# A state-space mixer's taps and state outputs on 32-column tiles of TensorE

## The chip, the cores and the metric

The kernel runs on one core of one Trainium2 chip. The metric is the device time of one execution, in microseconds; three runs of the kernel before took 1072.55, 1073.31 and 1074.68 us, median 1073.31 us.

## What is computed

The program is two transformer blocks over 256 tokens of width 1024: two layers of a first block (a state-space mixer, a gated spatial mixer, a differential attention, a conv-gated MLP), then one layer of a second block with three attention branches. The change touches only the state-space mixer of the first block:

```
def s5_mixer(u, a_re, a_im, log_dt, b_re, b_im, c_re, c_im, d_skip, w_glu, b_glu):
    ...
    a_bar = jnp.exp(lam * dt)
    b_bar = ((a_bar - 1.0) / lam)[..., None] * b_mat
    bu = jnp.einsum("bsgh,gph->bsgp", uf.astype(jnp.complex64), b_bar)
    ...
    _, states = lax.associative_scan(combine, (a_seq, bu), axis=1)
    y = jnp.real(jnp.einsum("bsgp,ghp->bsgh", states, c_mat))
    y = y + d_skip.astype(jnp.float32).reshape(SSM_GROUPS, SSM_GROUP) * uf
    y = jax.nn.gelu(y.reshape(bsz, seq, SSM_WIDTH))
    y = y * jax.nn.sigmoid(y @ w_glu.astype(jnp.float32) + b_glu.astype(jnp.float32))
```

There are 256 channels in 16 groups of 16; each group has 64 complex states of its own, and groups don't mix before the last product.

## The kernel before, in words

All weights stream from memory once, in a fixed order of use (`Stream`, L98). ACT writes the upper part of a weight tile (`whi`, L152), DVE the rest (`wlo`, L153), and TensorE (PE) multiplies three times per tile (L94, the helper `Bank.mm`: `xh*whi`, `xh*wlo`, `xl*whi`). The order of the instructions on each engine is made by a scheduler when the kernel is built, from the order of the code and from priorities; it is fixed in the program, and no engine overtakes itself.

The mixer takes segments of 4 tokens. `ssm_prep` (once per layer) makes its constants. The layer-0 call runs beside the first products, the layer-1 call beside the layer-0 MLP. For each half `a` (128 of the 256 channels, four groups of 32 channels, numbered `q`) it

- writes the powers of A times B, padded with zeros, into a tile `pad`, one for the real and one for the imaginary part (two copies of ACT each, L600);
- transposes `pad` on PE (L603) and copies it out into `bt` (ACT, L604);
- multiplies `pad` by C into the four taps of 128x128 (`px<-sgen,sgen`, helper L94), of which only the four diagonal blocks of 32x32 are not zero by construction and are kept: four copies of ACT into `ktap` (L616), and one DVE instruction that adds the skip term (L617).

All of this goes through one PSUM bank, `px` (a pool of one), so each step waits until the step before has been copied out.

`ssm_gen` runs the mixer: 16 small transfers spread the input over partitions (L896, queue SP), PE makes what each segment adds (L905), DVE scans over segments (L920) and makes the state before each segment (L409, L929). Then two sets of products go into one PSUM bank: taps times inputs (`acc<-ut,ktap`), and states times `ct` (`acc<-sgen,ct`, 64 products per layer, which the trace shows as 128 instructions). Each of the latter has 32 weight columns, writes 32 rows of the bank (`yv[rows, ...]`), and so takes one of four column tiles of PE. Their loop has the group `q` outside, and the tap `i` and the part `ri` inside, so eight products in a row go to the same column tile:

```
for q in range(4):
    rows = slice(q * 32, q * 32 + 32)
    j = a * 4 + q
    for i in range(4):
        for ri in range(2):
            yb.mm(yv[rows, a, i, :], ct[:, i, ri, j * 32 : j * 32 + 32], st_[ri][:, j, :],
```

ACT's gelu (L948) reads that bank when all are done, and PE's next step of the mixer (L954, the gate) reads the gelu.

The whole program is PE's 7751 matmul instructions and their weight loads, at 96% busy. A product of two fp32 operands stands in the trace as two instructions, one that is written with fp32r operands (the weight stream) as one.

Of the kernel before, what the change touches and what calls it, by code (L numbers as in the profile page):

```python
# [20 lines left out]
P = 128  # L21
# [18 lines left out]
# columns of the transposed parameter rows  # L40
AG, FG, GP, GM, SG, SD, BG, BM, AR, AI, GV, NPV = 0, 16, 32, 40, 48, 50, 54, 58, 82, 98, 114, 118
# columns of the constant table
# [3 lines left out]
def constant_table():  # L46
    """Rotary tables, masks: functions of shapes only. Tokens of block 2 stand in the order
    (t mod 4, t div 4 mod 4, t div 16)."""
# [30 lines left out]
@contextmanager  # L79
def later(tc, n):  # L80
    """Scheduled as if traced n instructions later."""
    tc.cur_priority += n
    yield
    tc.cur_priority -= n


class Bank:
    """One PSUM bank, whose accumulation groups share one start and one stop."""
# [4 lines left out]
    def mm(self, out, lhsT, rhs, stop=False):  # L93
        self.nc.tensor.matmul(out, lhsT=lhsT, rhs=rhs, start=not self.open, stop=stop)  # L94
        self.open = True


class Stream:  # L98
    """The weights in the order of their use: loaded, and split into two float32r parts, ahead of it."""
# [67 lines left out]
def tile_model(tc, t, out):  # L167
# [54 lines left out]
    # ------------------------------------------------------------------ weights in order of use  # L222
# [12 lines left out]
    # products of the mixers (lower case) and their generators' steps  # L235
# [58 lines left out]
    # ------------------------------------------------------------------ constants and small inputs  # L294
# [15 lines left out]
    def param_rows(*ps, eng=nc.sync):  # L310
        """Parameter rows -> columns of pvt."""
# [57 lines left out]
    # ------------------------------------------------------------------ small numeric helpers  # L369
    def rsqrt(src, n, scale, dst=None, tag=None):  # L370
        """1 / sqrt(src * scale + EPS) for a [P, n] tile."""
# [35 lines left out]
    # ------------------------------------------------------------------ first block: SSM parameters  # L407
# [12 lines left out]
    def ssm_params():  # L420
# [27 lines left out]
        # half angle -> full angle, then onto the unit circle  # L448
# [14 lines left out]
        # f = (a_bar - 1) / lambda  # L463
# [28 lines left out]
    def ssm_prep(l):  # L492
        """Segments of 4 tokens: A^i B-bar, C A^k, the 4-tap kernels Re(C A^i B-bar), the rotation table
        e^(-4 i theta m), m < 64, and the scan's multipliers."""
# [14 lines left out]
        def cmul(o, x, y, tv):  # L509
            """o = x * y for (re, im) pairs, tv scratch of o's shape."""  # L510
            tt(o[0], x[0], y[0], OP.mult)
            tt(tv, x[1], y[1], OP.mult)
            tt(o[0], o[0], tv, OP.subtract)
            tt(o[1], x[0], y[1], OP.mult)
            tt(tv, x[1], y[0], OP.mult)
            tt(o[1], o[1], tv, OP.add)
# [6 lines left out]
        # C^T, states on partitions, expanded with zeros and compact  # L523
# [15 lines left out]
        # powers of A, 0 to 4, and their products with f  # L539
# [23 lines left out]
        # C A^k, k from 1 to 4, the imaginary part negated  # L563
# [15 lines left out]
        # A^i B-bar; stacked as (channel, i) rows by states, and times C for the taps  # L579
# [12 lines left out]
        for a in range(2):  # L592
            pads = []
            for ri in range(2):
                pad = sgen()
                G.memset(pad, 0.0)
                pd = pad.rearrange("p (j h c i) -> p h j c i", j=4, i=4, h=2)
# [8 lines left out]
                yield  # L606
            kb = psx()
            for ri in range(2):
                cs = slice(ri * S + a * P, ri * S + (a + 1) * P)
                for i in range(4):  # L610
                    kb.mm(kb.t[:, i * P : (i + 1) * P], pads[ri].rearrange("p (k i) -> p k i", i=4)[:, :, i],
                          c0[:, cs], stop=ri == 1 and i == 3)
            kv = kb.t.rearrange("p (i c) -> p i c", i=4)
            for q in range(4):
                ps = slice(q * 32, q * 32 + 32)
                A.copy(ktap[ps, :, a, ps], kv[ps, :, ps])  # L616
# [3 lines left out]
        # rotation table  # L620
# [28 lines left out]
    # ------------------------------------------------------------------ token order of block 2  # L649
# [6 lines left out]
    # ------------------------------------------------------------------ normalisation helpers  # L656
# [5 lines left out]
    def split_scaled(hi, lo, src, scale):  # L662
        """hi + lo = src * scale, scale a [P, 1] column or a float."""
# [7 lines left out]
    class Stats:  # L671
        """Sums of squares over d (rows of the d-major tiles) per token."""
# [26 lines left out]
    def token_ss(src, n):  # L699
        """Sum of squares over the free axis of src[:, tt, :] (token-major), [P, 2]."""  # L700
# [11 lines left out]
    # ------------------------------------------------------------------ products  # L712
    low = [0]

    def mm_xs(X, banks, outs, sub, k0, kn, last):
        """Token-major: outs[tt] += X[:, k, tt].T @ W[k]."""
# [15 lines left out]
    def mm_ws(X, bank, outs, sub, k0, kn, last):  # L732
        """d-major: outs[n] += W[k][:, n].T @ X[:, k]."""
# [57 lines left out]
    # ------------------------------------------------------------------ x, its first norm  # L791
# [13 lines left out]
    # masks and rotary tables  # L805
# [11 lines left out]
    def rope_gain(pool, name, con, c0, s0, g, axes):  # L817
        """Tables with the norm's gain folded in: cos * g, and sin * (g of the other half)."""
# [68 lines left out]
    # ------------------------------------------------------------------ mixers of the first block  # L887
    def ssm_gen(l, ut, mix):
        tab, rr, bt, ct, wg = SSM[l]
        # ut: [P, (a, i, m)], token 4 m + i  # L890
# [3 lines left out]
        for q in range(4):  # L894
            for i in range(4):
                nc.sync.dma_start(u4v[3 - i : P : 4, q], utv[q * 32 : q * 32 + 32, :, i, :])  # L896
        yield
        w = [sgen(), sgen()]
        for a in range(2):
            # what each segment adds to its last state  # L900
# [21 lines left out]
        # state before each segment, from 0  # L922
# [15 lines left out]
        for a in range(2):  # L938
            for q in range(4):
                rows = slice(q * 32, q * 32 + 32)  # L940
                j = a * 4 + q
# [901 lines left out]
```

## Time and profile before

| | before |
|---|---|
| three runs, device time | 1072.55, 1073.31, 1074.68 us |
| span of the profiled execution (first to last instruction; the page gives no other time of it) | 1071.4 us |
| PE busy | 1028.5 us, 7751 instructions |
| DVE busy | 779.0 us |
| ACT busy | 624.1 us |
| DMA, mean over the span | 156 GB/s |

A busy time counts from an instruction's start to its end. PE's instructions overlap, and a wide one lasts 0.28 us though the next starts 0.12 us after it, so the distance of the starts, not the duration, says what an instruction costs. In the timeline a run of like instructions is one row, from the first start to the last end, with their number.

### The profile page before, as it was taken

The page shows a single profiled execution, that of the slowest core. Times are in us where ns is not written, and L with a number is a line of the kernel's source. Part 1 is how long each engine was busy: PE and PEld are TensorE (multiplying, and loading weights), DVE is VectorE, ACT ScalarE, POOL GpSimd, SP SyncE. Part 2 cuts the span into 40 slices and gives each one's busy share as a digit, 9 for nine tenths or more (in the row PEclk, how much of TensorE's full clock was granted, in tenths as well). Part 3 has the DMA queues.
Part 4 walks back from the last instruction along what each step waited for, and adds up shares of the span by engine and source line. Part 5 has one row for each costly group of instructions (what it writes and reads, how often), then busy time and mean ns, then how long its engine had stood idle before and what let it go on. Part 6 is the DMA issues. An engine that isn't in the chain of part 4 may idle for free.

```text
span 1071.4 us, 19616 instructions
## 1 busy us (share of the span) xinstructions
PE 1028.5 (96%) x7751; PEld 956.9 (89%) x7751; DVE 779.0 (73%) x1577; ACT 624.1 (58%) x1206; POOL 14.3 (1%) x34
## 2 busy tenths in 40 slices
PE   7799999999999999998999999999999999999994
PEld 5678898999999988888999999999787899899993
DVE  6978769877888769658878787876665666546663
ACT  5876567655665667657655555645675555444450
POOL 2000000000000000100000000000000000000000
PEclk9899999999999999999999999999999999999997
DMA  7542253555655445135556555468332546336531
GB/s 200 194 141 91 63 173 118 191 172 185 222 177 193 158 131 191 66 124 170 164 176 207 169 190 193 152 184 275 121 119 80 167 114 195 112 113 192 164 137 39
DMA packets 130484, 166.66 MB, mean 156 GB/s; under 512 B 12034, under 2 KB 103256, under 8 KB 130392
## 3 DMA queue, kind: packets, MB, share of 16 engines
q1 hardware_dynamic: 130360, 165.40, 47.9%
q8 instruction: 61, 1.00, 0.4%
q14 instruction: 31, 0.25, 0.1%
q10 hardware_dynamic: 32, 0.01, 0.0%
HBM read 160.15 MB, written 1.05 MB: 150 GB/s over the span
## 4 chain that ended last, share of the span: by engine, by line
PE 85%; DVE 7%; ACT 4%; issue 1%; DMA 1%; SPq 0%; POOL 0%; ACTq 0%; POOLq 0%; DVEq 0%
PE acc L94 50%; PE ps L94 26%; PE px L94 2%; DVE sgen L409 2%; DVE wlo L153 1%; PE pt L1506 1%; ACT sgen L600 1%; ACT whi L152 1%; ACT gen L1005 1%; PE px L905 1%; PE acc L1561 1%; DMA wraw<-in_w_in_dram 1%; PE acc L1652 1%; PE pt L1124 0%; DVE gen L1331 0%
## 5 line engine op out<-in xcount | busy, mean ns | idle before, releaser
L152 ACT ACTIVATE whi<-wraw 128x1024 fp32r<-128x1024 f32 x294 | 307.7, 1060 | 235.0 <-PE acc L94 112.5
L153 DVE TENSOR_TENSOR wlo<-wraw,whi 128x1024 fp32r<-128x1024 f32 x294 | 356.5, 1222 | 103.5 <-ACT whi L152 100.6
L94 PE MATMUL ps<-xh,whi 128*128 128x256 f32 x736 | 208.6, 285 | 3.7 <-DVE gen L1342 3.4
L94 PE MATMUL ps<-xl,whi 128*128 128x256 f32 x736 | 208.2, 283 | 0.8 <-DVE xl L665 0.8
L94 PE MATMUL ps<-xh,wlo 128*128 128x256 f32 x736 | 207.9, 283 | 0.0
L94 PE MATMUL acc<-xh,wlo 128*128 128x256 f32 x672 | 193.7, 289 | 4.0 <-DVE wlo L153 4.0
L94 PE MATMUL acc<-xh,whi 128*128 128x256 f32 x672 | 194.9, 291 | 1.2 <-ACT vm L1195 0.7
L94 PE MATMUL acc<-xl,whi 128*128 128x256 f32 x672 | 193.9, 289 | 0.5 <-DVE xl L669 0.5
L94 PEld LDWEIGHTS ps<-xh,whi 128*128 128x128 f32 x736 | 140.5, 191 | 4.4 <-DVE gen L1342 1.9
L94 PEld LDWEIGHTS ps<-xl,whi 128*128 128x128 f32 x736 | 140.8, 191 | 1.1 <-DVE xl L665 1.0
L94 PEld LDWEIGHTS ps<-xh,wlo 128*128 128x128 f32 x736 | 140.8, 191 | 0.0
L94 PEld LDWEIGHTS acc<-xh,wlo 128*128 128x128 f32 x672 | 129.6, 193 | 5.8 <-DVE wlo L153 4.7
L94 PEld LDWEIGHTS acc<-xh,whi 128*128 128x128 f32 x672 | 129.4, 193 | 4.7 <-issue 1.3
L94 PEld LDWEIGHTS acc<-xl,whi 128*128 128x128 f32 x672 | 129.5, 193 | 2.8 <-issue 1.5
L94 PE MATMUL acc<-whi,xh 128*128 128x512 f32 (+1 forms) x352 | 125.5, 358 | 3.0 <-ACT xh L664 2.6
L94 PE MATMUL acc<-wlo,xh 128*128 128x512 f32 (+1 forms) x352 | 125.8, 357 | 1.7 <-DVE wlo L153 1.6
L94 PE MATMUL acc<-whi,xl 128*128 128x512 f32 (+1 forms) x352 | 124.7, 355 | 0.0
L94 PE MATMUL acc<-al,whi 128*128 128x256 f32 x352 | 99.0, 281 | 0.5 <-DVE al L669 0.5
L94 PE MATMUL acc<-ah,whi 128*128 128x256 f32 x352 | 99.2, 282 | 0.0
L94 PE MATMUL acc<-ah,wlo 128*128 128x256 f32 x352 | 98.6, 281 | 0.0
L94 PEld LDWEIGHTS acc<-whi,xh 128*128 128x128 f32 x352 | 67.4, 191 | 11.7 <-ACT xh L664 3.5
L94 PEld LDWEIGHTS acc<-wlo,xh 128*128 128x128 f32 x352 | 67.4, 191 | 10.7 <-DVE wlo L153 2.6
(348 smaller groups left out, 1558.2 us busy)
## 6 DMA issues: line engine op xcount, KB each, us to landing
wraw<-in_w_in_dram SPq DMA_DIRECT2D x58, 1024.0 KB
wraw<-in_w_up_dram SPq DMA_DIRECT2D x44, 1024.0 KB
wraw<-in_w_down_dram SPq DMA_DIRECT2D x22, 1024.0 KB
wraw<-in_w_out_dram SPq DMA_DIRECT2D x12, 1024.0 KB
wraw<-in_w_mem_kv_dram SPq DMA_DIRECT2D x4, 1024.0 KB
gen<-gen SPq DMA_DIRECT2D x48, 64.0 KB
wraw<-in_w_br_b_dram SPq DMA_DIRECT2D x2, 1024.0 KB
wraw<-in_w_br_m_dram SPq DMA_DIRECT2D x2, 1024.0 KB
```

Source lines behind the costliest of these rows:

```text
L94: self.nc.tensor.matmul(out, lhsT=lhsT, rhs=rhs, start=not self.open, stop=stop)
L152: self.nc.scalar.activation(hv, part, AF.Copy)
L153: self.nc.vector.tensor_tensor(lv, part, hv.bitcast(F32), op=OP.subtract)
L409: (eng or V).tensor_tensor(o, a, b_, op=op)
L600: A.copy(pd[ps, hf], bpow[ri][ps, a * 4 : a * 4 + 4])
L905: T.matmul(bv[:, ri, q, :], lhsT=bt[:, ri, a, q * P : (q + 1) * P], rhs=u4[:, a * 4 + q, :], start=True, stop=True)
L1005: A.activation(sq[:, i * 64 : i * 64 + 64], src[:, i * 64 : i * 64 + 64], AF.Square, scale=rstd[:, q : q + 1], accum_out=ss[:, i : i + 1])
L1506: T.transpose(bk.t[:, i * P : (i + 1) * P], p[:, i * P : (i + 1) * P], ident)
L1561: T.matmul(oc, lhsT=pt[:, kt * P : (kt + 1) * P], rhs=vs[0][:, kt, cols], start=kt == 0, stop=False)
L1652: T.matmul(oc, lhsT=pt[:, (i * 2 + kt) * P : (i * 2 + kt + 1) * P], rhs=vb[:, kt, kv * 64 : kv * 64 + 64], start=kt == 0, stop=kt == 1)
```

## The change

The padded tile is laid out as (tap, channel) within each group of 32 channels, so that the 32 columns of one tap and one group lie side by side. The taps are made group by group: a product of 32 weight columns by 32 moving columns, written to the 32 rows of its group, with the four groups (column tiles) as neighbours. The state outputs get the same order: the group inside, tap and part outside. The 16 transfers of `ssm_gen` follow the new row order.

```
     def mm(self, out, lhsT, rhs, stop=False, start=None):
...
-                pd = pad.rearrange("p (j h c i) -> p h j c i", j=4, i=4, h=2)
+                pd = pad.rearrange("p (j i h c) -> p h j c i", j=4, i=4, h=2)
...
             kb = psx()
+            kv = kb.t[:, :P].rearrange("p (i c) -> p i c", i=4)
             for ri in range(2):
-                cs = slice(ri * S + a * P, ri * S + (a + 1) * P)
                 for i in range(4):
-                    kb.mm(kb.t[:, i * P : (i + 1) * P], pads[ri].rearrange("p (k i) -> p k i", i=4)[:, :, i],
-                          c0[:, cs], stop=ri == 1 and i == 3)
-            kv = kb.t.rearrange("p (i c) -> p i c", i=4)
+                    for q in range(4):
+                        ps = slice(q * 32, q * 32 + 32)
+                        c = ri * S + a * P + q * 32
+                        kb.mm(kv[ps, i, :], pads[ri][:, q * P + i * 32 : q * P + i * 32 + 32], c0[:, c : c + 32],
+                              start=ri == 0 and i == 0, stop=ri == 1 and i == 3)
             for q in range(4):
                 ps = slice(q * 32, q * 32 + 32)
-                A.copy(ktap[ps, :, a, ps], kv[ps, :, ps])
+                A.copy(ktap[ps, :, a, ps], kv[ps])
...
-                nc.sync.dma_start(u4v[3 - i : P : 4, q], utv[q * 32 : q * 32 + 32, :, i, :])
+                nc.sync.dma_start(u4v[(3 - i) * 32 : (4 - i) * 32, q], utv[q * 32 : q * 32 + 32, :, i, :])
...
         for a in range(2):
-            for q in range(4):
-                rows = slice(q * 32, q * 32 + 32)
-                j = a * 4 + q
-                for i in range(4):
-                    for ri in range(2):
-                        yb.mm(yv[rows, a, i, :], ct[:, i, ri, j * 32 : j * 32 + 32], st_[ri][:, j, :],
+            for i in range(4):
+                for ri in range(2):
+
+                    for q in range(4):
+                        j = a * 4 + q
+                        yb.mm(yv[q * 32 : q * 32 + 32, a, i, :], ct[:, i, ri, j * 32 : j * 32 + 32], st_[ri][:, j, :],
                               stop=a == 1 and i == 3 and ri == 1)
```

The rest of the diff takes comments out and shifts later line numbers by three.

**What moves.** Counted over the program, 32 products of 128x128 give way to 128 of 32x32 on PE, and the 16 copies L600 of ACT get another shape; every other instruction is there as before. The scheduler moves some: on PE all but two blocks of the differences lie between rows 179 and 500, the mixers of layer 0 (the two are the layer-1 taps); on DVE they lie between rows 196 and 546, on ACT between 62 and 244; on SP one load changes places, on POOL nothing does.

PE, the first taps of layer 0 (`px_642` is the bank of the taps, `px_660` and after the change `px_684` the next transposes through the same bank; an order row of x4 holds four products). Before:

```order
L94 MATMUL acc_895<-xh_160,wlo_709 128x256
L94 MATMUL px_642<-sgen_429,sgen_529 128x128 x4
L94 MATMUL px_642<-sgen_429,sgen_539 128x128 x4
L94 MATMUL acc_1026<-wlo_749,xh_160 128x512
L94 MATMUL acc_1026<-whi_748,xl_161 128x512
L94 MATMUL acc_1027<-whi_748,xh_160 128x512
L94 MATMUL acc_1027<-wlo_749,xh_160 128x512
L94 MATMUL acc_1027<-whi_748,xl_161 128x512
L94 MATMUL acc_1026<-whi_748,xh_160 128x512
L603 MATMUL px_660<-ident,sgen_656 128x128 x4
```

And now:

```order
L94 MATMUL acc_943<-xh_160,wlo_757 128x256
L94 MATMUL px_642<-sgen_429,sgen_529 32x32 x16
L94 MATMUL px_642<-sgen_429,sgen_539 32x32 x16
L94 MATMUL acc_1074<-wlo_797,xh_160 128x512
L94 MATMUL acc_1074<-whi_796,xl_161 128x512
L94 MATMUL acc_1074<-whi_796,xh_160 128x512
L94 MATMUL acc_1074<-wlo_797,xh_160 128x512
L603 MATMUL px_684<-ident,sgen_680 128x128 x4
```

The taps stand in the same place as one closed block, and the transposes behind them come after four wide products in place of six.

ACT, around the copies out of that bank (`ktap`). Before:

```order
L604 COPY bt_420<-px_543 128x512
L600 COPY sgen_684<-sgen_503 64x4x64 x2
L152 ACTIVATE whi_1046<-wraw_924 128x1024
L616 COPY ktap<-px_642 32x4x32 x4
L604 COPY bt_420<-px_660 128x512
L604 COPY bt_420<-px_688 128x512
L152 ACTIVATE whi_1062<-wraw_924 128x1024
L616 COPY ktap<-px_694 32x4x32 x4
L1001 ACTIVATE gen_779<-acc_624,rstd_209 128x512
```

And now:

```order
L604 COPY bt_420<-px_543 128x512
L600 COPY sgen_708<-sgen_503 64x4x16x4 x2
L619 COPY ktap<-px_642 32x4x32 x4
L152 ACTIVATE whi_1094<-wraw_972 128x1024
L604 COPY bt_420<-px_684 128x512
L604 COPY bt_420<-px_712 128x512
L152 ACTIVATE whi_1110<-wraw_972 128x1024
L619 COPY ktap<-px_718 32x4x32 x4
L152 ACTIVATE whi_1128<-wraw_1092 128x1024
L1004 ACTIVATE gen_827<-acc_624,rstd_209 128x512
```

The first four copies of `ktap` now stand ahead of the weight split instead of behind it, and one more split stands ahead of the k-norm (L1001, now L1004).

PE, the start of the state outputs of layer 0 (`acc_1481`, after the change `acc_1529`, is their bank; `sgen_1467` and `sgen_1468`, now `sgen_1515` and `sgen_1516`, are the two parts of the states). Before:

```order
L94 MATMUL acc_1571<-xl_1257,whi_1163 128x256
L94 MATMUL acc_1571<-xh_1256,wlo_1164 128x256
L94 MATMUL acc_1481<-sgen_1468,ct 32x64
L94 MATMUL acc_1481<-sgen_1467,ct 32x64
L94 MATMUL acc_1481<-sgen_1468,ct 32x64
```

And now:

```order
L94 MATMUL acc_1619<-xh_1304,whi_1211 128x256
L94 MATMUL acc_1529<-sgen_1515,ct 32x64 x4
L94 MATMUL acc_1619<-xl_1305,whi_1211 128x256
L94 MATMUL acc_1619<-xh_1304,wlo_1212 128x256
L94 MATMUL acc_1529<-sgen_1516,ct 32x64 x4
L94 MATMUL acc_1529<-sgen_1515,ct 32x64 x4
```

Four products with the same part, one for each column tile, now stand together where one stood.

## Rows read from the trace of the kernel before

**Rows 1.** The page: span, and the engines' busy time.

```profile
span 1071.4 us, 19616 instructions
...
PE 1028.5 (96%) x7751; PEld 956.9 (89%) x7751; DVE 779.0 (73%) x1577; ACT 624.1 (58%) x1206; POOL 14.3 (1%) x34
```

**Rows 2.** Stretches (us): length, busy time of each engine, PE clock, DMA share, GB/s.

```profile
55.00:70.00 15.00, 15.00 (x74) 13.38 (x73) 10.21 (x32) 8.29 (x22) 0.53 (x1) 1.00 0.37 124
...
75.00:100.00 25.00, 24.82 (x173) 21.57 (x173) 22.20 (x88) 19.35 (x65) 0.00 (x0) 1.00 0.42 145
...
216.00:344.00 128.00, 128.00 (x1074) 127.75 (x1074) 103.35 (x170) 79.67 (x120) 0.00 (x0) 1.00 0.56 185
```

**Rows 3.** Timeline of PE, first taps: start, duration, line, operation, count.

```profile
55.55 0.28 PE L94 MATMUL acc<-xh,wlo 128*128 128x256 f32 x1
55.80 4.00 PE L94 MATMUL px<-sgen,sgen 128*128 128x128 f32 x16
59.55 0.48 PE L94 MATMUL acc<-wlo,xh 128*128 128x512 f32 x1
```

**Rows 4.** Groups by line and shape on PE: busy us, mean ns, idle before.

```profile
L94 PE MATMUL px<-sgen,sgen 128*128 128x128 f32 x64 | 15.8, 400 | 0.2 <-ACT bt L604 0.2
L94 PE MATMUL acc<-sgen,ct 128*32 128x64 f32 x256 | 12.1, 221 | 0.0
```

**Rows 5.** Stretches inside the state outputs, PE alone: instructions in flight or started.

```profile
119.25:119.30 0.05, 0.05 (x3) 1.00 0.00 0
119.25:119.64 0.39, 0.39 (x9) 1.00 0.00 0
119.73:119.76 0.03, 0.03 (x5) 1.00 0.00 0
119.73:119.92 0.19, 0.19 (x11) 1.00 0.00 0
```

**Rows 6.** Timeline of PE: two 64-column tiles side by side, in ever longer windows.

```profile
760.27 0.28 PE L1561 MATMUL acc<-va,gen 128*128 128x64 f32 x1
760.48 0.27 PE L1563 MATMUL acc<-vw,gen 128*64 128x64 f32 x1
...
760.48 0.28 PE L1563 MATMUL acc<-vw,gen 128*64 128x64 f32 x2
...
760.48 0.34 PE L1563 MATMUL acc<-vw,gen 128*64 128x64 f32 x4
760.74 0.38 PE L94 MATMUL acc<-wlo,xh 128*128 128x256 f32 x1
```

**Rows 7.** Timeline of PE: state outputs of layer 0 and of layer 1, and what follows.

```profile
119.13 5.87 PE L94 MATMUL acc<-sgen,ct 128*32 128x64 f32 x126
124.93 0.66 PE L1148 MATMUL pt<-ident,gen 128*128 128x128 f32 x4
...
425.67 5.98 PE L94 MATMUL acc<-sgen,ct 128*32 128x64 f32 x128
431.58 0.33 PE L1119 MATMUL pt<-ident,gen 128*128 128x128 f32 x1
...
433.74 1.89 PE L954 MATMUL px<-sgen,wglu 128*128 128x256 f32 x8
```

**Rows 8.** Waits from 54 to 76 us: engine and line, for whom, total, times, longest.

```profile
ACT ktap L616 <- PE px L94: 4.8, 2, 3.1
```

**Rows 9.** Timeline of DVE in layer 0 and of ACT in layer 1.

```profile
121.15 1.29 DVE L409 TENSOR_TENSOR gen<-gen,sm 128x512 f32<-128x512 f32 x2
...
428.14 1.28 ACT L948 ACT_TABLE_LOAD   x1
431.69 0.60 ACT L948 ACTIVATE sgen<-acc 128x512 f32<-128x512 f32 x1 [2.27 <-PE acc L94]
```

**Rows 10.** Copies of ACT (busy, mean ns), and DVE's stepped write (min/median/max ns).

```profile
L600 ACT COPY sgen<-sgen 64x256 f32<-64x256 f32 x16 | 10.5, 654 | 1.2 <-POOL sgen L596 1.0
L1054 ACT COPY kz<-pt 64x256 f32<-64x256 f32 x8 | 2.9, 368 | 0.1
...
L409 DVE TENSOR_TENSOR ut<-acc,rstdB x4: 602/620/629, 57.2 to 387.4; 128x256 f32<-128x256 f32 x4
```

More of the change, by code (lines that the diff above doesn't have):

```diff
@@ L91, in __init__, with mm @@
         self.nc, self.t, self.open = nc, t, False
-    def mm(self, out, lhsT, rhs, stop=False):
-        self.nc.tensor.matmul(out, lhsT=lhsT, rhs=rhs, start=not self.open, stop=stop)
+    def mm(self, out, lhsT, rhs, stop=False, start=None):
+        self.nc.tensor.matmul(out, lhsT=lhsT, rhs=rhs, start=not self.open if start is None else start, stop=stop)
         self.open = True
```

## The prediction

> **What bounds the kernel now.** I read the page first. PE is busy for 1028.5 of 1071.4 us, and no other engine comes near [rows 1], so an instruction less on PE counts wherever the others keep up. Whether they do is read from the stretches [rows 2]. In the layer-0 MLP (216 to 344 us) PE works all 128.00 us, DVE 103.35, ACT 79.67: PE sets the pace and the others have room. In the mixers of layer 0 PE is full from 55 to 70, but from 75 to 100 DVE has 22.20 of 25 us, so a gain there can run into DVE. PE's clock is granted in full (1.00, the 2.4 GHz level) in each of these stretches and in those of rows 5, so it changes none of the prices. Then I read the timeline of PE at the two places that the change rewrites, the distances of starts inside them, and last what stands behind them on PE, DVE and ACT.
>
> **The taps.** One block of taps is 16 instructions. From the start of the last wide product before it to that of the next one behind it 59.55 - 55.55 = 4.00 us pass [rows 3]. The four blocks are alike: 15.8 us busy over 64 instructions [rows 4]. Inside, the starts are (4.00 - 0.40)/15 = 0.24 us apart. After the change a block has 64 instructions of 32 by 32. Their distance p isn't in the trace and has to be bounded.
> - One column tile alone takes a 64-column instruction every 57 ns: the stretch that is 0.34 us longer holds six more (the first two rows of [rows 5]). An instruction of 32 columns should not cost more. If time goes with the columns, it is 28 ns per tile.
> - Do column tiles run side by side? Two rows say yes. Where the state outputs pass from one tile to the next, six instructions start in 0.16 us, 27 ns apart, so two tiles at 57 ns run at once (the last two of [rows 5]). And two 64-column tiles of the second block start within 0.01 us of each other, weights and all: one instruction up to 760.48, two up to 760.49 [rows 6].
> - So p is 28/4 = 7 ns with four tiles at once. That is also about the distance of the two starts in rows 6, the shortest that I can see. The upper ends are 28 ns (one instruction at a time, each as long as a tile needs) and 57 ns (nothing gained by fewer columns or by tiles). I take 7 ns, because rows 6 are the nearest: fp32, column tiles as neighbours, one bank.
> - Going to column tiles and back costs time too: 760.48 - 760.27 = 0.21 us from the last full product to the first narrow one; and the last narrow start (0.25 us before the end of the group at 760.82, so 760.57) stands 0.17 us before the next full one [rows 6]. With the first weight load, 0.4 us a block.
>
> A block then takes 0.4 + 64 x 0.007 = 0.85 us, 3.1 less than 4.00. At 28 ns it is 2.2 (1.8 less), at 57 ns 4.0 (nothing).
>
> **The state outputs.** A layer has 128 instructions, (5.98 - 0.22)/127 = 45 ns apart in layer 1 and (5.87 - 0.22)/125 = 45 ns in layer 0 [rows 4, 7]. 45 lies below 57 because neighbouring groups overlap at each change of tile [rows 5]. With the tiles as neighbours, four at once give 57/4 = 14 ns, and 127 x 0.031 = 3.9 us less per layer. At 28 ns it is 2.2 us, at 45 ns nothing. The way into the column tiles and out of it is paid now as then.
>
> **What of it reaches the end.**
> - The two blocks in the layer-0 MLP: all, 6.2 us, since PE is the bound there [rows 2].
> - The two blocks in the mixers of layer 0, worth 6.2 on PE: ACT waits 4.8 us for them [rows 8], the transposes behind them need the same bank, and now the copies out stand ahead of the weight split, so the chain shortens with PE. But DVE is near its own bound soon after [rows 2], and the scheduler has shuffled this part. I take three quarters, 4.7; the bounds are 3 and 6.2.
> - The state outputs of layer 0, worth 3.9: the next on PE are four transposes, which need what DVE makes from 121.15 on; the first of those two instructions is done half way, at 121.8 [rows 9]. PE would be done at 119.13 + 128 x 0.014 + 0.2 = 121.1, and the transposes start at 121.8 instead of 124.93 [rows 7]: 3.1.
> - The state outputs of layer 1, worth 3.9: PE has other work from 431.58 to 433.74, then the gate L954 [rows 7], which needs the gelu. ACT waits 2.27 us for the state outputs, and can't begin the gelu before its table load ends at 428.14 + 1.28 = 429.42; then the gelu takes 0.60, to 430.02, and PE would be at the gate at 429.84 [rows 7, 9]. With some slip for the scores in between, 3.5.
>
> **What the change adds.** The padded copies L600 now write at a step of 32 elements, in place of runs of 64. They take 654 ns where an even copy of the same size takes 368, because they read at a step already [rows 10]. DVE's stepped write of 128x256 takes 0.62 us, so a stepped write costs on the order of a stepped read [rows 10]. If read and write run together, the copy stays at 654 ns; if they add, up to 0.65 us more each. Five copies stand ahead of the first block on ACT, so the bounds are 0 and 3.3 us there; the eight of layer 1 are under the MLP, where ACT has 48 us free [rows 2]. I take 0, because reading and writing are two streams of one instruction. The 16 transfers L896 keep number and bytes, and only the target rows change: 0, bounds 0.5 either way. PE gets 192 instructions more, inside p. The eviction of `ktap` keeps its shape: 0. The shuffled order in layer 0 I put at 0, bounds 2 us either way.
>
> **The sum.** 6.2 + 4.7 + 3.1 + 3.5 = 17.5 us. The trace is one execution of span 1071.4; the median of the runs is 1.9 us above it, for what lies around the span, and that stays. 1073.3 - 17.5 = **1055.8 us**.
>
> **Rivals.**
> - *One weight load at a time.* The load of the next tile waits for that of this one, p is 28 ns at both places. Taps 1.8 a block: 3.6 in the MLP, 2.7 in the mixers; state outputs 2.2 in each layer (PE is done after DVE's row there): 10.7, so 1062.6 us. For it: the 27 ns of rows 5 could be such a limit as well as two tiles at work. Against it: the second start of rows 6. The Trainium skill ("TensorE: Matmul & The Clock Gate", Part 3: Packing small matmuls) says that a weight load overlaps running matmuls only where the row group differs; column tiles share all rows, so by that rule this rival would come true; the trace disagrees where the second narrow product starts within 0.01 us of the first. The same page (section "Wait — 56ns, not 53.3ns?") puts the floor between two starts at about 25 ns; by it a block would take 2.0 us and the program about 1062 us, and again rows 6 disagree, though only over two instructions.
> - *The mixers of layer 0 keep their length.* DVE sets the pace from 75 to 122 us, and both gains ahead of it are lost but for 1 us: 6.2 + 3.5 + 1 = 10.7, again 1062.6. For it: DVE's 89% from 75 to 100. Against: DVE and ACT themselves wait for the taps. Together with the first rival: 3.6 + 2.2 + 1 = 6.8, 1066.5.
> - *Nothing runs side by side.* p is 57 ns for the taps and 45 to 57 for the states: the change doesn't do what it says, and the time is 1073 us. Rows 5 and 6 speak against it.
> - *Each change of tile drains PE* (slower). If every step to the neighbour cost 0.2 us, as the step from the full array to column tiles does [rows 6], a block would take 32 x 0.2 + 64 x 0.028 + 0.4 = 8.6 us, 4.6 more, and the states of a layer 64 x 0.2 + 128 x 0.045 = 18.6, 12.7 more: 44 us more at most, about 1115 us. It decides from some 0.03 us per change on, where the 256 changes eat what 28 ns saves (4 x 1.8). Against it: rows 5 show no gap at a change of tile, and rows 6 none between neighbours.
>
> **How the numbers follow.** Forecast 0.66; loads one at a time 0.18; mixers keep their length 0.11; nothing side by side 0.03; drain 0.02. The first three are faster, by far more than 0.2% (2.1 us, about what a measurement of this kernel can tell from no change): faster 0.95, same 0.03, slower 0.02. Low end: all that PE saves arrives (6.2 + 6.2 + 3.9 + 3.9 = 20.2) and the new order gives 2 us more, 1051. High end: both middle rivals, 1066.
>
> **What would show it.** In the profile after: a tap block of about 0.9 us between its wide neighbours, 64 instructions some 7 ns apart; a layer's state outputs in some 2.0 us; ACT's wait for `ktap` nearly gone; a small new wait of PE for DVE ahead of L1148 (now L1151). L600 longer than 0.7 us, starts 25 to 28 ns apart, or a layer-0 MLP that begins less than 5 us earlier would show where it is wrong.

## The result and the profile after

The changed kernel took 1059.5 us (median of four runs, 1058.25 to 1060.28) against 1073.05 us before: ratio 0.9867, 95% interval 0.9853 to 0.9881, so 13.6 us or 1.3% faster. Forecast were 1055.8 us, 17.5 us less, in a range of 1051 to 1066. The direction and the range held; the gain came out 3.9 us smaller.

The page of the changed kernel, answering to [rows 1]:

```profile
span 1056.5 us, 20003 instructions
...
PE 1008.0 (95%) x7943; PEld 934.4 (88%) x7943; DVE 778.8 (74%) x1577; ACT 624.6 (59%) x1206; POOL 14.3 (1%) x34
```

PE has 192 instructions more and is busy 20.5 us less. The span is 14.9 us shorter, so PE's idle time has grown by 5.6 us. The timeline of PE at the rewritten places (first taps; state outputs of layer 0 and what follows; the wide product behind the second taps of the layer-0 MLP; state outputs of layer 1), answering to [rows 3, 7]:

```profile
55.34 0.28 PE L94 MATMUL acc<-xh,wlo 128*128 128x256 f32 x1
55.59 0.76 PE L94 MATMUL px<-sgen,sgen 128*32 128x32 f32 x64
56.28 0.50 PE L94 MATMUL acc<-wlo,xh 128*128 128x512 f32 x1
...
113.99 0.32 PE L94 MATMUL acc<-sgen,ct 128*32 128x64 f32 x8
...
115.24 1.88 PE L94 MATMUL acc<-sgen,ct 128*32 128x64 f32 x120 [0.51 <-DVE sgen L409]
118.64 0.63 PE L1151 MATMUL pt<-ident,gen 128*128 128x128 f32 x4 [1.52 <-DVE gen L409]
119.17 1.99 PE L957 MATMUL px<-sgen,wglu 128*128 128x256 f32 x8
...
201.01 0.39 PE L94 MATMUL ps<-xh,whi 128*128 128x256 f32 x1
...
414.15 1.99 PE L94 MATMUL acc<-sgen,ct 128*32 128x64 f32 x128
...
418.56 2.00 PE L957 MATMUL px<-sgen,wglu 128*128 128x256 f32 x8 [0.16 <-ACT sgen L951]
```

A block of taps goes from 4.00 us between its wide neighbours to 56.28 - 55.34 = 0.94 us, the state outputs of layer 1 from 5.98 to 1.99 us. The prices of PE were about right; what is behind them is read from the starts. Stretches of PE that begin at the first start of a block (lengths are rounded to 0.01 us):

```profile
186.24:186.26 0.02, 0.02 (x4) 1.00 0.05 0
186.24:186.29 0.05, 0.05 (x4) 1.00 0.08 20
186.24:186.30 0.06, 0.06 (x6) 1.00 0.07 17
```

Four instructions start within 0.02 us. They must be one for each column tile, since on a single tile the next start comes 31 to 53 ns later (one_tile, below); the next four come only when the first tile is free again. Behind the first round, the starts of single instructions come in rounds of four every 32 ns in the taps (32 columns) and every 56 ns in the state outputs (64 columns); over a block the mean distance is 9.0 and 14.0 ns.

Where the lead of the changed kernel over the one before arises, from the start of the same instruction in both timelines ([rows 3, 7], the rows above, and these three of the kernel before):

```profile
117.64 0.30 PE L94 MATMUL acc<-sgen,ct 128*32 128x64 f32 x2
...
125.69 1.99 PE L954 MATMUL px<-sgen,wglu 128*128 128x256 f32 x8
...
212.26 0.36 PE L94 MATMUL ps<-xh,whi 128*128 128x256 f32 x1
```

| place | before | after | lead, us | forecast gain | gain |
|---|---|---|---|---|---|
| layer 0, last wide product ahead of the first taps | 55.55 | 55.34 | 0.21 | 0 | 0.21 |
| layer 0, first state output | 117.64 | 113.99 | 3.65 | 4.7 (taps in the mixers) | 3.4 |
| layer 0, gate (L954, now L957) | 125.69 | 119.17 | 6.52 | 3.1 | 2.9 |
| wide product behind the second taps of the MLP | 212.26 | 201.01 | 11.25 | 6.2 | 4.7 |
| layer 1, first state output | 425.67 | 414.15 | 11.5 | 0 | 0.3 |
| layer 1, gate | 433.74 | 418.56 | 15.2 | 3.5 | 3.7 |

The first 0.21 us have nothing to do with the taps: the start-up of two executions differs by more than that even for one kernel (0.8 us between the two profiled executions of the change). So two terms fell short: the taps in the mixers by 1.3 us and the taps in the MLP by 1.5 us. In this profiled execution 14.9 of 17.5 us were gained; the other 1.3 us of the 3.9 lie between this execution, the fastest of the four, and their median (below).

**The MLP.** The waits of PE from 184 to 200 us in the changed kernel, and ACT's timeline there:

```profile
PE px L603 <- issue: 0.7, 1, 0.7
PE px L94 <- ACT bt L604: 0.3, 1, 0.3
```

```profile
186.21 1.09 ACT L1333 ACTIVATE gen<-gen,cvt 128x256 f32<-128x256 f32 x2
187.21 1.99 ACT L152 ACTIVATE whi<-wraw 128x1024 fp32r<-128x1024 f32 x2
189.11 0.61 ACT L1348 ACTIVATE gen<-gen 128x512 f32<-128x512 f32 x1
189.63 1.05 ACT L619 COPY ktap<-px 32x128 f32<-32x128 f32 x4
```

The taps are done at 187.0, but in ACT's order two conv steps, two weight splits and a gelu stand ahead of the copies, as they did before. It copies the taps out from 189.63 to 190.68. The transposes (L603) need the same bank and wait until 190.78. ACT, which had waited 0.55 us for PE here, is now the one that is waited for. The taps themselves wait 0.3 us for the same bank, until ACT has copied out the transposes ahead of them (`bt`).

**The mixers of layer 0.** Before, DVE waited twice for the copies of `ktap`, 2.7 us together (waits from 54 to 76 us):

```profile
DVE ktap L617 <- ACT ktap L616: 2.7, 2, 1.7
```

In the changed kernel these waits are gone, and DVE, not PE, is the engine that never pauses (columns as in [rows 2], where from 55 to 70 us PE had 15.00 and DVE 10.21 of 15 us):

```profile
57.00:72.00 15.00, 13.59 (x126) 9.81 (x125) 15.00 (x47) 12.19 (x39) 0.00 (x0) 1.00 0.32 93
```

DVE's first row of this stretch stands at 56.99, in the kernel before at 57.09. So no more than about the 2.7 us of waiting could be gained on DVE there: its L409 row `gen<-gen,gen` behind the second `ktap` goes from 69.11 to 66.11, 3.0 us, while PE's wide product behind the second taps goes from 67.46 to 62.07, 5.4 us. On ACT the weight split that now stands ahead of the k-norm (L1004) waits 1.63 us for PE, and the k-norm comes 2.85 us earlier. Which of the two, DVE's full stretch or ACT's new order, would be the bound without the other isn't shown.

Later PE waits 1.52 us ahead of L1151. The chain of work up to there, in the changed kernel (start, us, what):

```profile
114.42 0.17 DVE sm L373
...
115.27 1.13 DVE wlo L153
...
117.80 0.70 DVE gen L409
```

DVE's small dependent steps (the norm of the attention output), with a weight split among them, end at 118.5; the row that stood at 121.15 [rows 9] stands at 117.80, only 3.35 us earlier.

ACT's row for the copies of `ktap` (busy us, mean ns, idle before), which bears on a smaller claim:

```profile
L619 ACT COPY ktap<-px 32x128 f32<-32x128 f32 x16 | 4.1, 254 | 0.2
```

The padded copies with the stepped write (L600) have a mean of 690 ns in the same view, 36 ns more a copy (654 before, [rows 10]). ACT's idle time ahead of the copies of `ktap`, of which [rows 8] show 4.8 us from 54 to 76 us, is 0.2 us in all.

### The profile page after: what moved, and what is told of

Its sections match the earlier page's. It is cut to its first block, busy times and chain, and to the rows that moved or that the text cites. A ratio compares the mean times of both kernels' runs of the same rounds, so it can differ in the third digit from the quotient of the medians.

```text
span 1056.5 us, 20003 instructions
## 1 busy us (share of the span) xinstructions
PE 1008.0 (95%) x7943; PEld 934.4 (88%) x7943; DVE 778.8 (74%) x1577; ACT 624.6 (59%) x1206; POOL 14.3 (1%) x34
## 3 DMA queue, kind: packets, MB, share of 16 engines
q8 instruction: 62, 1.02, 0.4%
## 4 chain that ended last, share of the span: by engine, by line
PE 79%; DVE 4%; ACT 3%; issue 1%; SPq 0%; DMA 0%; POOL 0%; ACTq 0%; POOLq 0%
PE acc L94 47%; PE ps L94 26%; DVE wlo L153 1%; PE pt L1509 1%; ACT whi L152 1%; PE px L94 1%; PE acc L1564 1%; PE acc L1655 1%; DVE sgen L409 1%; ACT sgen L600 1%; DVE gen L1334 0%; ACT gen L1008 0%; DVE gen L1336 0%; DVE gen L409 0%; PE acc L1566 0%
```

## The experiments

**taps_only and states_only.** The two halves of the change alone:

```diff
-            for i in range(4):
-                for ri in range(2):
-                    for q in range(4):
+            for q in range(4):
+                for i in range(4):
+                    for ri in range(2):
```

That is taps_only, the changed kernel with its state outputs in the old order; states_only is the kernel before with the same lines the other way round.

Expected of taps_only:

> The change with the state outputs in their old order (group outside). Theory (each part earns what its own place in the trace shows: 4.7 us in the layer-0 MLP, 3.7 us in the mixers of layer 0 up to the state outputs): 8.4 us faster than before, about 1064.7 us, state outputs again 45 ns apart. Rival (the gain in layer 0 comes from the state outputs and the new order alone, DVE keeping the length of the mixers): only the 4.7 us, about 1068.4 us.

Expected of states_only:

> The kernel before with the state outputs alone in the new order. Theory (parts add up): 3.5 us in layer 1 and 2.9 us in layer 0, where PE then waits for DVE's row behind it: 6.4 us faster than before, about 1066.7 us. Rival (in layer 0 DVE gives none of it): 3.5 us, about 1069.6 us.

Measured against 1073.02 us: taps_only 1067.54 us (ratio 0.9949, 0.9937 to 0.9962), states_only 1066.69 us (0.9944, 0.993 to 0.9957). The state outputs gave what was expected, the taps only 5.5 of 8.4 us, and the sum, 11.8 us, is less than the 13.6 of both together. (These 1.8 us are not clear of noise by the times alone: each of the three intervals is 2.6 to 3 us wide. The traces have to say what is in them.) In the trace of taps_only the MLP gives 4.0 us in spite of a drop of the clock that cost 1.44 (below), of which 0.67 had come back by 184 us, while the mixers give 4.0 us up to the last state outputs, but only 2.7 at the gate. There PE waits (PE and ACT in taps_only):

```profile
120.90 0.66 PE L1150 MATMUL pt<-ident,gen 128*128 128x128 f32 x4
122.98 1.99 PE L956 MATMUL px<-sgen,wglu 128*128 128x256 f32 x8 [1.43 <-ACT sgen L950]
```

```profile
121.04 1.28 ACT L950 ACT_TABLE_LOAD   x1 [6.79 <-issue]
122.33 0.60 ACT L950 ACTIVATE sgen<-acc 128x512 f32<-128x512 f32 x1
```

ACT loads the gelu's table only after the state outputs have ended. In the kernel before, that load ran from 117.63 on, while they were still being computed. The two programs differ in what the load waits for (before, then taps_only):

```
L948 ACT_TABLE_LOAD [waits DVE_49]
L948 ACTIVATE sgen_1554<-acc_1481 128x512 [waits PE_49]

L950 ACT_TABLE_LOAD [waits DVE_49,PE_49]
L950 ACTIVATE sgen_1602<-acc_1529 128x512 [waits Activation_49]
```

The gelu's output tile is another one in the new order, and the gelu now waits for ACT itself too. In the listing the wait for ACT has taken the place on the gelu, and the wait for PE has moved to the table load ahead of it.

**taps_gelu.** taps_only with the gelu written over a tile whose last reader is PE:

```diff
-        yg = sgen()
+        yg = st_[0].rearrange("p j m -> p (j m)")
```

Expected of taps_gelu:

> The new taps with the old order of state outputs, as in taps_only, and the gelu writing over the first state tile as in own_bank_gelu. Theory (in taps_only the table load of the gelu stood behind the state outputs of layer 0 and cost PE 1.43 us ahead of the gate): the load starts before the state outputs end, the gate starts about 1.3 us after their end instead of 2.2 us or more, and all that follows is 1.2 to 1.4 us earlier than in taps_only. Rival (the gate waits for DVE's work as well): unchanged.

ACT and PE in taps_gelu:

```profile
113.38 1.28 ACT L950 ACT_TABLE_LOAD   x1
120.12 0.60 ACT L950 ACTIVATE sgen<-acc 128x512 f32<-128x512 f32 x1 [5.46 <-PE acc L94]
```

```profile
120.02 0.66 PE L1150 MATMUL pt<-ident,gen 128*128 128x128 f32 x4
120.77 1.99 PE L956 MATMUL px<-sgen,wglu 128*128 128x256 f32 x8
```

The load is back ahead of the wait, and the gate starts 0.75 us after the transposes in place of 2.08: the theory holds, 1.33 us. In one run it took 1064.66 us, 2.9 us less than taps_only's median; the trace shows 1.33 of it here. The rest is no effect of the gelu: this execution stood 0.95 us ahead of the profiled one of taps_only at the first taps (the wide product behind them at 55.24 against 56.19), and it has one drop of the clock where that one has two. In the changed kernel the same late load is there (117.23, after the state outputs), but DVE's chain covers nearly all of it.

**wide_even, strided_narrow and one_tile** take the tap block apart; two of them try other orders of the state outputs as well.

In wide_even the layout is new and the products are 128x128; the weight columns lie side by side, but belong to other taps (the loop bounds and the copies out are cut here):

```diff
-                    for q in range(4):
-                        ps = slice(q * 32, q * 32 + 32)
-                        c = ri * S + a * P + q * 32
-                        kb.mm(kv[ps, i, :], pads[ri][:, q * P + i * 32 : q * P + i * 32 + 32], c0[:, c : c + 32],
-                              start=ri == 0 and i == 0, stop=ri == 1 and i == 3)
...
+                    kb.mm(kb.t[:, i * P : (i + 1) * P], pads[ri][:, i * P : (i + 1) * P],
+                          c0[:, cs], stop=ri == 1 and i == 3)
```

In strided_narrow the products are new and the layout is the old one, with a weight column every 4 elements (the rest of the edit, cut here, sets the padded layout and the transfers back):

```diff
-                        kb.mm(kv[ps, i, :], pads[ri][:, q * P + i * 32 : q * P + i * 32 + 32], c0[:, c : c + 32],
+                        kb.mm(kv[ps, i, :], pads[ri].rearrange("p (j c i) -> p j c i", j=4, i=4)[:, q, :, i], c0[:, c : c + 32],
```

In one_tile the loop is turned, so that 16 instructions in a row go to one column tile:

```diff
-            for ri in range(2):
-                for i in range(4):
-                    for q in range(4):
+            for q in range(4):
+                for ri in range(2):
+                    for i in range(4):
```

Expected of wide_even:

> The new padded layout, but the taps as 32 products of 128x128 again, each with 128 weight columns side by side; it leaves out which columns belong to which tap, so the taps are other values. State outputs: tap outside, then group, then part, so that a product's neighbour is on the same tile twice before the next tile. Theory A (the step of the weights made the old block slow): starts about 0.11 us apart, 2.1 us a block, so the layout alone earns 1.9 of the 3.0 us and the column tiles the rest. Theory B (a 128x128 fp32 product takes 0.233 us whatever the layout): 4.0 us as before. State outputs: between 14 and 45 ns apart, 30 ns as an estimate between the two orders measured.

Expected of strided_narrow:

> Taps as 32x32 products on neighbouring column tiles, but from the old padded layout, so that a product's 32 weight columns lie 4 elements apart; padded copies and transfers as before. State outputs in pairs of column tiles (groups 0 and 1, then 2 and 3). Theory A (the old block was slow because its weights were read at a step, about 58 ns for 32 columns, one read at a time): 64 x 0.058 = 3.7 us a block, little gained over 4.0. Theory B (only the product's time counts, and tiles run side by side): 0.95 us as with the change. State outputs: if a tile is busy 56 ns per instruction and two run at once, 28 ns apart, 3.6 us a layer; if the order of issue limits, nearer to 45 ns.

Expected of one_tile:

> The changed kernel with the taps' loop turned: group outside, part and tap inside, so that 16 instructions in a row go to the same column tile. Theory (a tile is busy 32 ns with 32 columns, as the distance of one group of four to the next shows, and only neighbours on other tiles overlap): 64 x 0.032 + 0.35 = 2.4 us a block in place of 0.95. Rival 1 (an instruction on one tile costs 57 ns whatever its columns): 3.9 us. Rival 2 (the order of the tiles does not matter, the narrow products do): 0.95 us.

The first tap block in the timeline of PE, in wide_even:

```profile
55.76 0.28 PE L94 MATMUL acc<-xh,wlo 128*128 128x256 f32 x1
56.00 2.05 PE L94 MATMUL px<-sgen,sgen 128*128 128x128 f32 x16
57.81 0.48 PE L94 MATMUL acc<-wlo,xh 128*128 128x512 f32 x1
```

In strided_narrow, and its state outputs of layer 1 in pairs of tiles:

```profile
54.16 0.28 PE L94 MATMUL acc<-xh,wlo 128*128 128x256 f32 x1
54.41 1.20 PE L94 MATMUL px<-sgen,sgen 128*32 128x32 f32 x64
55.53 0.50 PE L94 MATMUL acc<-wlo,xh 128*128 128x512 f32 x1
...
414.79 3.21 PE L94 MATMUL acc<-sgen,ct 128*32 128x64 f32 x128
```

And in one_tile:

```profile
54.49 0.28 PE L94 MATMUL acc<-xh,wlo 128*128 128x256 f32 x1
54.73 1.91 PE L94 MATMUL px<-sgen,sgen 128*32 128x32 f32 x64
56.57 0.50 PE L94 MATMUL acc<-wlo,xh 128*128 128x512 f32 x1
```

| taps | first block, neighbour to neighbour |
|---|---|
| 128x128, weights every 4 elements (before) | 4.00 us |
| 128x128, weights side by side (wide_even) | 2.05 us |
| 32x32, one tile after the other (one_tile) | 2.08 us |
| 32x32, four tiles, weights every 4 elements (strided_narrow) | 1.37 us |
| 32x32, four tiles, weights side by side (the change) | 0.94 us |

Theory A is right for the old block: with the weights side by side the starts are 112 to 118 ns apart in place of 233 to 240, and two thirds of the gain come with the layout alone, before any column tile. Narrow products on one tile at a time gain nothing beyond that (one start every 27 ns on average); four tiles at once give the last 1.1 us. For strided_narrow neither theory held: the step still costs, but on four tiles at once, a round of four takes 60 ns in place of 32. Theory A's 3.7 us supposed one read at a time. The Trainium skill ("SBUF — State Buffer", section "Specifications (TRN2)") says that the lines there have 16 bytes, that full bandwidth needs at least two hits per line and that each cross to a new line pays. Weights four fp32 elements apart take a new line each, and both comparisons agree (233 against 112 ns, 60 against 32 ns); that the lines are the reason is not shown by itself.

The state outputs in pairs take 3.34 us from neighbour to neighbour (3.6 expected), two starts every 56 ns, as expected for two tiles at once, and a little less where one pair of tiles gives way to the next. The order "tap, group, part" of wide_even takes 2.06 us (the change 1.99), 14.5 ns a start, hardly more than the 14.0 of the change, where 30 was my estimate: a neighbour on the same tile in between costs next to nothing here. In one run each, wide_even took 1062.24, strided_narrow 1061.33, one_tile 1061.16 us.

**after_again and own_bank_gelu.** The changed kernel once more, and a version in which the layer-1 taps have a bank that the MLP leaves unused (with the gelu's tile as in taps_gelu). Every engine's order stays.

```diff
-            kb = psx()
+            kb = pst() if l else psx()
```

Expected of after_again:

> The changed kernel once more, unaltered, to see how its time spreads with the granted clock. Theory (its median lies above its first profiled execution, 1058.25 us, because in most executions the clock falls to its lower level for about 3 us somewhere in the middle, which costs 1.4 us): runs in steps, at 1058.3 us with a mean clock of 0.993 and near 1059.7 us with 0.990, median 1059.5 us. Rival (plain scatter): times unrelated to the granted clock.

Expected of own_bank_gelu:

> The changed kernel with two waits taken away: the layer-1 taps go to the bank of the transposes (pt), which the MLP leaves unused, so that the next transposes (L603) need not wait for the copies of ktap; and the gelu writes over the first state tile in place of a fresh one, so that it waits for PE alone and its table load stands ahead of that wait. The order on every engine is that of the changed kernel. Theory: the 0.9 us that PE waits in the layer-0 MLP and the 0.2 us ahead of the gate in layer 0 go: 1.1 us faster than the changed kernel, about 1058.4 us median. Rival (the wait moves on to ACT's copy of bt, which stands in the same queue): 0 to 0.2 us.

Measured against 1073.08 us: after_again 1059.85 us (ratio 0.9875, 0.986 to 0.989), own_bank_gelu 1058.54 us (0.9861, 0.9845 to 0.9878). The intervals overlap, so the times alone don't tell the two apart. The traces do. PE's timeline in own_bank_gelu (the gate of layer 0, the first taps of the MLP, the transposes, the wide product behind the second taps):

```profile
119.15 1.89 PE L957 MATMUL px<-sgen,wglu 128*128 128x256 f32 x8
...
185.72 0.76 PE L94 MATMUL pt<-sgen,sgen 128*32 128x32 f32 x64
189.40 0.60 PE L603 MATMUL px<-ident,sgen 128*128 128x128 f32 x4
...
199.61 0.39 PE L94 MATMUL ps<-xh,whi 128*128 128x256 f32 x1
```

Both waits of PE from 184 to 200 us are gone, the transposes come at 189.40 in place of 190.78 though ACT copies `ktap` when it did before (189.60), and the MLP's share of the lead grows from 4.7 to 6.1 us (212.26 - 199.61 less 125.69 - 119.15). So the shared bank, with ACT's order behind it, was the cost. In layer 0 the early table load changed nothing (the gate at 119.15 against 119.17), as DVE's chain covers it. Its median is the lowest of the versions that compute the same result, though not clear of the changed kernel's; its profiled execution has a drop of the clock at 490 us that the first one of the change has not.

Of the spread, that such drops come and cost about 1.4 us where they fall holds in the traces; the steps do not: after_again's four runs were at 1058.32 (mean clock 0.991), 1059.18, 1060.53 and 1060.6 (0.990 each), no two steps. What a drop looks like, in taps_only (stretch, length, PE, PE clock, DMA share, GB/s):

```profile
158.00:161.00 3.00, 1.75 (x14) 1.00 1.08 365
161.00:162.00 1.00, 0.46 (x2) 0.72 1.10 349
162.00:163.00 1.00, 1.00 (x7) 0.50 0.75 224
163.00:164.00 1.00, 1.00 (x6) 0.50 0.00 0
164.00:165.00 1.00, 1.00 (x7) 0.58 0.00 0
```

PE had waited 1.7 us for the norm of the MLP, and the granted clock falls to the 1.2 GHz level for 3.4 us (0.56 + 1 + 1 + 0.84, from these rows); the lead over before falls by 1.44 us. The profiled execution of the change waited as long at that place and shows 1.00 throughout. Such a drop stands in taps_only twice, in wide_even, strided_narrow, taps_gelu, own_bank_gelu and after_again once, in pool_tab twice and in no_scale once, and between the first 51 us and the last products in neither profiled execution of the first comparison. In after_again it came at 157 us, and its execution was still as fast as the first: it had begun 0.9 us sooner, and 0.66 of the 1.47 us that the drop cost had come back by 180 us, where PE then waited less for ACT. So a drop does not always cost its full price. That the median lies 1.25 us above the profiled run of 1058.25 fits this, but only profiled executions show their clock by place; for the others it stays open.

**pool_tab and no_scale** were to show that DVE bounds the end of layer 0's mixers.

In pool_tab the doubling of the table `tab` in layer 0 goes to POOL (`gtt` is the same operation there):

```diff
-                 sgen().rearrange("p (j n) -> p j n", j=8)[:, :, :c])
+                 sgen().rearrange("p (j n) -> p j n", j=8)[:, :, :c],
+                 tt=gtt if l == 0 else tt)
```

In no_scale the norm's multiplication is left out in layer 0:

```diff
-            tt(ov_, ov_, rs[:, q * 4 : q * 4 + 4].unsqueeze(2).to_broadcast([P, 4, P]), OP.mult)
+            if l:
+                tt(ov_, ov_, rs[:, q * 4 : q * 4 + 4].unsqueeze(2).to_broadcast([P, 4, P]), OP.mult)
```

Expected of pool_tab:

> own_bank_gelu with 34 of DVE's small instructions of layer 0 (the doubling of the table tab, about 8 us of DVE between 57 and 80 us) given to POOL, which is nearly idle; the scheduler reorders the mixers of layer 0 for it. Theory (in layer 0 DVE keeps back 1.5 us of what PE saves: PE waits that long for DVE ahead of the transposes L1151): with DVE freed, PE's wait there shrinks below 0.5 us and the gate of layer 0 comes 1 to 1.5 us earlier than in own_bank_gelu, about 1057.3 us. Rival (it is the chain of small dependent steps just ahead of the transposes, not DVE's load before them): the wait stays at 1.5 us, and the time at 1058.5 us; POOL's own slowness can also delay the first use of the table, and then PE waits at L908 or DVE at its first product with tab.

Expected of no_scale:

> own_bank_gelu without DVE's two multiplications of the attention's output by its norm in layer 0 (L409, gen<-gen,sm), so that the transposes of that output read what ACT has copied out; it leaves out that scaling, and PE's transposes come ahead of the last state outputs. Theory (the chain of DVE's small steps and those two rows keeps back the end of layer 0's mixers: PE waits 1.5 us for it): that wait goes, the state outputs are followed by the gelu and the gate at once, and the layer-0 MLP begins 1.2 to 1.5 us earlier than in own_bank_gelu. Rival (PE was late there for want of something else, ACT's copies or the states themselves): less than 0.3 us.

pool_tab took 1067.36 us (ratio 0.9946, 0.9932 to 0.9959), 8.8 us more than own_bank_gelu. Its longest wait of PE from 55 to 130 us says why:

```profile
PE px L886 <- DMA gen<-in_gmlp_w_s_dram: 5.9, 1, 5.9
```

The scheduler moved the order in the mixers, and a load of weights came 5.9 us too late for PE; behind that wait the granted clock is at the 1.2 GHz level from 84.0 to 90.9 us. The wait ahead of the transposes (there L1155) is 0.2 us, but all ahead of it had come later, so of DVE this tells nothing. no_scale (1058.3 us in one run, with other values) takes away the wait at L1151 and the 0.5 us ahead of the second run of state outputs, but what follows came only 0.4 us earlier (the wide product behind the second taps of the MLP at 199.21 against 199.61). Its largest waits of PE from 112 to 145 us:

```profile
PE pt L1152 <- DVE xl L668: 0.4, 1, 0.4
PE acc L94 <- ACT xh L667: 0.2, 1, 0.2
```

The state outputs stand in three pieces there in place of two, each with its way into the column tiles and out of them, and three smaller waits, 0.8 us together, take the place of the large one. So the row that releases PE in the trace is right, but taking it away in this order earned about a quarter of the 1.5 us; neither the theory's 1.2 to 1.5 us nor the rival's 0.3 us came out. How much is DVE's and how much the new order's isn't separated.

## Why the prediction was right in the main, and where it was too large

- **The price of the narrow products: about right.** I took 7 ns between starts and 0.85 us a block; it is 9.0 ns and 0.90 to 1.02 us (1.32 where PE waits for `bt`). The second figure behind it, 28 ns for 32 columns on one tile, is 32. For the state outputs 14 ns was forecast and 14.0 measured. Rows 6, two neighbours 0.01 us apart, were the right nearest rows. "The four blocks are alike" was a little off: the old blocks take 4.00, 3.89, 4.19 and 3.77 us from neighbour to neighbour, so PE saves 11.7 us on them in place of 12.4.
- **Loads one at a time, nothing side by side, drain per change: refuted.** Four starts within 0.02 us leave no room for them. So the two rules of the Trainium skill ("TensorE: Matmul & The Clock Gate") that the prediction weighed ("Part 3: Packing small matmuls", loads overlap only where the row group differs; "Wait — 56ns, not 53.3ns?", a floor of about 25 ns between starts) don't hold for neighbouring column tiles here, where the starts are 6 to 7 ns apart and 9.0 ns on average. On one tile the starts in one_tile are 31.7 ns apart, above that floor.
- **State outputs of layer 1: right**, 3.5 forecast, 3.7 measured at the gate; the gelu starts at 417.91 right behind its table load, as the chain that I added up from rows 7 and 9 has it.
- **State outputs of layer 0: nearly right**, 3.1 against 2.9 at the gate (2.6 at the transposes, for which the sum was made), with the forecast wait of PE ahead of L1151 (1.52 us, where the sum has 0.7).
- **"The two blocks in the layer-0 MLP: all, 6.2 us, since PE is the bound there": this step failed**, by 1.5 us. The stretch that I read, 216 to 344 us [rows 2], begins behind both blocks, which lie from 192 to 212 us; PE was as full there (25.85 of 26 us from 190 to 216), but the copies out stand at a fixed place in ACT's order, behind 3.4 us of other work, which the taps' 4 us had covered. I asked who was busy in the stretch, not when ACT would come to the copies if PE were done at once. own_bank_gelu shows it: with a bank apart, the MLP's share is 6.1 us.
- **"I take three quarters, 4.7" for the mixers of layer 0** was still too much: 3.4 us. "ACT waits 4.8 us for them" was the wrong wait to go by: DVE waited only 2.7 us for the same copies, and with these gone it is busy without a pause from 57 to 72 us. The rival that the mixers keep their length came true in part, and earlier than it said, not from 75 us on. The new order of ACT ahead of the k-norm, put at 0, may have its part in it. That DVE's work is the whole cause is not shown: pool_tab could not test it, and no_scale, at the end of the mixers, freed 0.4 us.
- **The early order of the copies** ("now the copies out stand ahead of the weight split") did what it said: in layer 0 the copies follow the taps within 0.7 us.
- **What was left out:** the two sides of the median. The median was taken to lie 1.9 us above the profiled span, as before. After the change it lies 3.0 above (1059.5 against 1056.5), since the execution profiled was the fastest of its four. That is luck of the draw, and why the others were slower stays open.

## What to carry to other kernels

Look at the step of the weights before narrowing a product: an even layout alone took the block from 4.00 to 2.05 us, and neighbouring column tiles from there to 0.94. When a block gets short, look up at which place in its own order the engine that empties its bank stands; the time that the long block had covered comes to light there, and here a bank of its own gave it back (1.4 of 1.5 us). Where a second engine waits for the same block, its own waits are the most that it can gain. After any change of order compare the waits too: one more semaphore on an instruction of ACT can put a 1.28 us table load behind the wait that it used to run under.

## Not expected

- A 128x128 fp32 product whose weight columns lie four elements apart costs 233 ns a start, side by side 112; and on column tiles the step costs too (60 in place of 32 ns a round), but on four tiles at once.
- The table load that moved behind the state outputs through one more wait of the gelu (1.33 us in taps_only).
- The granted clock fell behind a 1.7 us wait of PE in some profiled executions and stayed up in others at the same place, 1.4 to 1.5 us each time.
- POOL took 0.61 to 0.95 us for elementwise operations of 128x248 that took DVE 0.41 us.
